# The products with the values in a chunk-band attention: by query tile of four heads instead of by pairs of heads

## The chip, the cores and the metric

The kernel runs on one core of a Trainium2 chip. The metric is the device time of one execution in microseconds. TensorE (PE) does the products and the transposes; its loads of stationary operands are shown apart (PEld). VectorE (DVE), ScalarE (ACT) and GpSimd (POOL) compute, and SyncE (SP) issues most DMAs. Each engine works through its own list of instructions in the order in which it stands and waits on semaphores for the others.

## The reference

One layer of a hybrid encoder on 1024 tokens of width 1024. Both mixers read one normalised input and one combined projection. The first is an attention of 8 heads of width 64 over a band of the own chunk of 64 tokens and the 8 chunks before it, with a learned bias by distance; the second a gated delta rule of 4 heads of width 128, a recurrence over chunks. Then come an output projection and a feed-forward part. Cut to what matters here:

```
scores = einsum('bcqhd,bckhd->bchqk', qc, kb) * Dh**-0.5 + bias
scores = where(valid, scores, finfo(float32).min)
p = softmax(scores, axis=-1)
o = einsum('bchqk,bckhd->bcqhd', p, vb)          # the products with the values
...
h = h + concat([rms_norm(o_att), o_dn]) @ w_out
h = h + square(relu(rms_norm(h) @ w_ff1)) @ w_ff2
```

## The kernel before, in words

The span falls into three parts: projections (to about 365 us), the two mixers side by side (365 to 575 us), and the output projection and feed-forward part (from 575 us, L931 and later), whose large products take more than half of the span.

In the middle part three generators are run in turns by `interleave` (L263): the attention (L706), `delta_all` (the recurrence, L687) and the rest of the projection of the values. A generator yields the TensorE time that it has just put down, and the one that lies furthest back goes next. That gives the program's order; within it a scheduler sets each engine's list by priority, by a simulated timeline: what comes earlier in the program has the higher priority, and what isn't ready is passed by something behind it. The list of an engine is thereby fixed when the kernel is built. `tc.issue_after(x)` keeps what is put down inside it from being placed ahead of the instruction x; `tc.high_priority()` puts what is inside ahead of everything else that is ready.

The attention works by group g of four heads (two groups) and query tile t of 128 tokens (eight tiles): 16 units, named t00 to t17 in the program's names. Each is worked in two pairs of heads, pp = 0 and 1, with e the head of the pair:

- `start` (L761) has q of the tile loaded (two DMAs on SP, two buffers).
- `score` (L797) makes the products q k of one pair (L793): one PSUM bank for the newest keys of both heads (t_sb), one for each head's older keys (t_sa); VectorE adds bias and finds the maximum (L808, L817), ScalarE takes exp (L823, L826). The results are t_pb (both heads) and t_pa (one for each head).
- `value` (L831) turns them so that keys lie on the partitions: transposes of t_pb (L844, t_tpb), copied by ScalarE (L847, t_tb); transposes of t_pa (L855, t_tpa), copied by ScalarE for e = 0 (L860) and by VectorE for e = 1 (L858). Then the products with the values (L865, t_o): for each key tile j and each head one product with 64 columns of stationary values, so that the two heads of a pair write the two halves of the partitions of one PSUM bank. In the trace each product is two records, and 128*64 is the part of the array that it uses.
- `finish` (L869) copies t_o (L884), transposes it back (L887) and scales it by the sums (L888; in the second group also L893, L895), and `turn` (L898) makes the finished tile the left operand of the output projection (L904).

Before, the loop (L908) goes over 32 pairs: scores of one pair, then the values of the pair before it, and after the second pair `finish`. The transposes go through two PSUM banks (`ps_t`), the scores through three (`ps_a`), the products with the values through one (`ps_o`).

The delta part has names c_ and m_: c_pk, c_pv, c_pq, c_pS, c_mt and c_po are its full-size products (L461), c_tpv, c_tpq and c_tpo its transposes (L465); m_p and m_tp (L568 to L592) are small products on 32 or 64 rows and columns.

Of the kernel before, what the change touches and what calls it, by code (L numbers as in the profile page):

```python
# [14 lines left out]
P = 128  # L15
# [3 lines left out]
NT = SEQ // P  # L19
# [27 lines left out]
def hymba_kernel(  # L47
# [20 lines left out]
    nc = tc.nc  # L68
# [16 lines left out]
    def page(tag, name, dt=F32, w=512):  # L85
        return pools[tag].tile([P, w], dt, tag=tag, name=name, bufs=slots[tag])
# [14 lines left out]
    def bank(pool, name):  # L101
        return pool.tile([P, 512], F32, tag="bk", name=name)
# [380 lines left out]
    turned = [[], []]  # L483
# [7 lines left out]
    def delta_prep(kT, ab):  # L491
# [54 lines left out]
        for dst, src in ((x_dr, xd), (y_dr, ad)):  # L546
            for h in range(4):
                nc.sync.dma_start(out=dst[:, :, h, :], in_=src.rearrange("(q h) r e -> h q r e", h=4)[h])

    def delta_merge(c, res):  # L550

        n = f"m{c}"
# [153 lines left out]
    def attention(after):  # L706
# [54 lines left out]
        def start(g, t):  # L761
            n = f"t{g}{t}"
            T = dict(n=n, k0=max(0, t - 4))
            T["kb"] = max(0, t - 1)
            if (g, t) == (1, 1):
                T["q"] = [page("on", f"{n}_q{m}", F32R) for m in range(2)]
                for r0 in (0, 64):
                    for m in range(2):
                        nc.sync.dma_start(out=T["q"][m].bitcast(F32)[r0:r0 + 64], in_=q_dr[t, :, m, g, :])
            else:  # L770
                q = page("x", n + "_q", F32R, w=DM)
                qf = q.bitcast(F32)
                for r0 in (0, 64):
                    nc.sync.dma_start(out=qf[r0:r0 + 64].rearrange("p (m c) -> p m c", m=2), in_=q_dr[t, :, :, g, :])
                T["q"] = [part(q, m) for m in range(2)]
            T["sums"] = small("t", n + "_sum", 8)
            T["nm"] = small("t", n + "_nm", 8)
            T["s"] = {}
            tiles[g, t] = T
# [48 lines left out]
            T["s"][pp] = sa, sb  # L828
            return cost

        def value(g, t, pp):  # L831
            T = tiles[g, t]
            n, k0, kb = (T[k] for k in ("n", "k0", "kb"))
            na, nb = kb - k0, t + 1 - kb
            if pp == 0:
                T["po"] = bank(ps_o, n + "_o")
            po = T["po"]
            sa, sb = T["s"].pop(pp)
            T["spare"] = sb
            tp = bank(ps_t, f"{n}_tpb{pp}")  # L840
            for e in range(2):
                for j in range(nb):
                    c = e * 256 + 256 - (nb - j) * P
                    nc.tensor.transpose(tp[:, c:c + P], sb[:, c:c + P], ident)  # L844
            tb = page("raw", f"{n}_tb{pp}", w=516)
            w3 = [t_[:, 0:512].rearrange("p (a b) -> p a b", a=2)[:, :, 256 - nb * P:256] for t_ in (tb, tp)]
            nc.scalar.copy(*w3)  # L847
            ta = [None, None]
            if na:
                for e in range(2):  # L850
                    i = 2 * pp + e
                    tp = bank(ps_t, f"{n}_tpa{i}")
                    for j in range(na):
                        js = slice(j * P, (j + 1) * P)
                        nc.tensor.transpose(tp[:, js], sa[e][:, js], ident)  # L855
                    ta[e] = page("u", f"{n}_ta{i}")
                    if e:
                        turned[1].append(nc.vector.tensor_copy(ta[e][:, 0:na * P], tp[:, 0:na * P]).ins)  # L858
                    else:
                        turned[0].append(nc.scalar.copy(ta[e][:, 0:na * P], tp[:, 0:na * P]).ins)  # L860
            for j in range(na + nb):
                for e in range(2):
                    h = 4 * g + 2 * pp + e
                    c = j * P if j < na else e * 256 + 256 - (na + nb - j) * P
                    nc.tensor.matmul(po[64 * e:64 * e + 64, pp * P:(pp + 1) * P], vt[k0 + j][:, 64 * h:64 * h + 64],  # L865
                                     (ta[e] if j < na else tb)[:, c:c + P], start=(j == 0), stop=(j == na + nb - 1))
            return (na + nb) * 650

        def finish(g, t):  # L869
            T = tiles.pop((g, t))  # L870
# [34 lines left out]
                                    bc_row(again), ALU.mult)  # L905
            return 500

        units = [(g, t, pp) for g in range(2) for t in range(NT) for pp in range(2)]  # L908
        lag, late = 1, 2
        for i in range(len(units) + lag + late):  # L910
            if i < len(units):
                g, t, pp = units[i]
                if pp == 0:
                    start(g, t)
                    if (g, t) == (0, 2):
                        load_rest()
                    if (g, t) == (0, 6):
                        load_new(1)
                        load_old(1)
                yield score(g, t, pp)  # L920
            if lag <= i < len(units) + lag:
                g, t, pp = units[i - lag]
                yield value(g, t, pp)
                if pp:
                    yield finish(g, t)
            if i >= lag + late:
                g, t, pp = units[i - lag - late]
                if g and pp:
                    yield turn(t)

    def out_proj():  # L931
# [476 lines left out]
```

## Time and profile before

| | |
|---|---|
| median of 3 runs | 1288.59 us (1287.44 to 1289.28) |
| profiled execution | 1288.31 us |
| its span | 1286.6 us |
| TensorE busy | 1260.6 us, 98% |
| VectorE busy | 935.0 us, 73% |
| ScalarE busy | 553.9 us, 43% |
| granted TensorE clock, mean | 0.998 |

The profile is one execution. A busy TensorE is one that has records under way; matmuls overlap, and a record's duration is its passage through the pipeline. What a record costs is seen in the distance between the starts of neighbours. Times in the views are in microseconds from the start of the span. In brackets behind a row stands the idle time ahead of it on its engine and what ended it.

### The profile page before, as it was taken

What the parts mean: (1) busy time and instruction counts of PE and PEld (TensorE: products, weight loads), DVE (VectorE), ACT (ScalarE), POOL (GpSimd) and SP (SyncE); (2) the same over time, 40 slices, a digit from 0 to 9 for tenths busy, and PEclk for the clock granted to TensorE, in tenths of its full rate; (3) what the DMA queues carried; (4) which work ended last, traced back from release to release, by engine and by line L of the source; (5) the groups of instructions that cost most, each with busy time, mean ns of one, the idle gap of its engine ahead of it and who ended that gap; (6) DMA issues with size and microseconds to landing.
All of it is one profiled execution on the core that took longest, in us unless ns stands there. A gap on an engine that the chain in (4) does not pass through costs nothing.

```text
span 1286.6 us, 18043 instructions
## 1 busy us (share of the span) xinstructions
PE 1260.6 (98%) x6702; PEld 1040.6 (81%) x6702; DVE 935.0 (73%) x1401; ACT 553.9 (43%) x919; POOL 293.0 (23%) x499
## 2 busy tenths in 40 slices
PE   9999999999999999989999999999999999999998
PEld 7778878788888887868877788888887888888886
DVE  7899987665046666863529876776668997897988
ACT  7233132133166664665335445444455443333331
POOL 4435461454024355523310000000000000000034
PEclk9999999999999999999999999999999999999999
DMA  6214353656492742125351433232358733422002
GB/s 223 61 44 140 100 164 112 145 147 160 144 270 79 218 109 75 42 65 163 122 166 31 151 116 129 98 110 97 105 196 318 238 93 104 131 86 95 17 33 98
DMA packets 129288, 160.65 MB, mean 125 GB/s; under 512 B 22832, under 2 KB 71984, under 8 KB 128688
## 3 DMA queue, kind: packets, MB, share of 16 engines
q1 hardware_dynamic: 111104, 137.20, 34.7%
q10 hardware_dynamic: 18096, 22.29, 5.0%
q8 instruction: 53, 0.87, 0.3%
q14 instruction: 35, 0.29, 0.1%
HBM read 111.75 MB, written 47.71 MB: 124 GB/s over the span
## 4 chain that ended last, share of the span: by engine, by line
PE 72%; DVE 8%; issue 2%; DMA 2%; POOL 1%; ACT 1%; POOLq 1%; SPq 0%; ACTq 0%; DVEq 0%
PE q L1087 22%; PE p L1183 20%; PE op L166 5%; PE av_ps L166 3%; PE aq_ps L166 3%; PE g_ps L166 3%; PE t_o L865 3%; PE ak_ps L166 2%; PE t_sb L793 1%; PE t_sa L793 1%; PE t_tpb L844 1%; PE t_tpa L855 1%; PE c_mt L461 1%; PE c_pS L461 1%; DVE ml L148 1%
## 5 line engine op out<-in xcount | busy, mean ns | idle before, releaser
L1255 POOL TENSOR_TENSOR y<-y,y 128x1024 f32<-128x1024 f32 x6 | 19.3, 3243 | 591.7 <-DVE y L1251 572.9
L1251 DVE TENSOR_TENSOR y<-y,p 128x1024 f32<-128x1024 f32 x46 | 55.2, 1218 | 5.4 <-PE p L1183 4.5
L808 DVE CUSTOM_DVE_ANT_0 t_pb<-t_sb,biasn 128x256 f32<-128x256 f32 (+1 forms) x64 | 25.4, 402 | 43.6 <-POOL biasn L720 25.4
L166 PE MATMUL op<-mh,wo_h 128*128 128x512 f32 x128 | 50.3, 393 | 0.8 <-DVE t_nm L808 0.3
L166 PE MATMUL op<-ml,wo_h 128*128 128x512 f32 x128 | 50.1, 391 | 0.0
L166 PE MATMUL op<-mh,wo_l 128*128 128x512 f32 x128 | 48.3, 391 | 0.0
L823 ACT ACTIVATE t_pb<-t_pb,t_nm 128x256 f32<-128x256 f32 (+1 forms) x64 | 31.6, 494 | 22.7 <-DVE t_nm L817 12.7
L966 DVE TENSOR_TENSOR h<-op,op_x 128x512 f32<-128x512 f32 x16 | 10.8, 688 | 30.7 <-PE op L166 30.7
L793 PE MATMUL t_sb<-ks,t_q 128*128 128x256 f32 (+1 forms) x144 | 30.4, 308 | 0.8 <-DMA t_q<-q_dr 0.5
L973 POOL TENSOR_TENSOR op_q<-op_q 128x512 f32<-128x512 f32 x14 | 20.1, 1439 | 48.0 <-ACT op_q L972 47.8
L166 PEld LDWEIGHTS op<-mh,wo_h 128*128 128x128 f32 x128 | 24.0, 188 | 7.4 <-issue 1.0
L817 DVE CUSTOM_DVE_ANT_0 t_pa<-t_sa,biaso,t_nm 128x384 f32<-128x384 f32 (+2 forms) x48 | 26.3, 547 | 4.4 <-PE t_sa L793 2.9
L865 PE MATMUL t_o<-t_ta,vt 128*64 128x128 f32 x240 | 27.3, 293 | 1.4 <-DVE t_ta L858 1.1
L166 PEld LDWEIGHTS op<-mh,wo_l 128*128 128x128 f32 x128 | 24.0, 188 | 5.2 <-issue 0.2
L166 PEld LDWEIGHTS op<-ml,wo_h 128*128 128x128 f32 x128 | 24.0, 188 | 4.9
L166 PE MATMUL g_ps<-uh,wg_h 128*128 128x512 f32 x64 | 25.2, 394 | 1.4 <-ACT wg_h L147 1.4
L826 ACT ACTIVATE t_pa<-t_pa,t_nm 128x384 f32<-128x384 f32 (+2 forms) x48 | 26.4, 550 | 0.1
L793 PE MATMUL t_sa<-ks,t_q 128*128 128x256 f32 (+2 forms) x128 | 25.5, 310 | 0.3 <-DVE t_nm L808 0.3
L166 PE MATMUL g_ps<-uh,wg_l 128*128 128x512 f32 x64 | 25.2, 394 | 0.4 <-POOL wg_l L148 0.4
L166 PE MATMUL dq_ps<-uh,wdq_h 128*128 128x512 f32 x64 | 25.5, 398 | 0.0
L166 PE MATMUL dv_ps<-uh,wdv_l 128*128 128x512 f32 x64 | 25.4, 397 | 0.0
L166 PE MATMUL aq_ps<-waq_h,uh 128*128 128x512 f32 x64 | 25.3, 401 | 0.0
(1102 smaller groups left out, 4353.8 us busy)
## 6 DMA issues: line engine op xcount, KB each, us to landing
wa<-in_w_ff_dram SPq DMA_DIRECT2D x32, 512.0 KB
a<-in_w_ff_dram SPq DMA_DIRECT2D x32, 512.0 KB
b<-f_dr SPq DMA_DIRECT2D x32, 512.0 KB
f_dr<-yy ACTq DMA_DIRECT2D x16, 512.0 KB
t_q<-q_dr SPq DMA_DIRECT2D x30, 256.0 KB
f_dr<-zz ACTq DMA_DIRECT2D x13, 512.0 KB
ks<-k_dr SPq DMA_DIRECT2D x16, 256.0 KB
wo_r<-in_w_out_dram SPq DMA_DIRECT2D x16, 256.0 KB
```

The source lines that it names most:

```text
L166: nc.tensor.matmul(ps, a, b, start=(i == 0), stop=(i == n - 1))
L461: nc.tensor.matmul(ps[:, hs], lhs(h, hs), rhs(h, hs), start=True, stop=True)
L793: nc.tensor.matmul(o, q[m][:, i * P:(i + 1) * P], k[:, c], start=(m == 0), stop=(m == 1))
L808: nc.vector.tensor_tensor_reduce(sb[:, c], bk[:, c], new[g][pp][:, c], -1.0, 3.0e38, ALU.add, ALU.min, nm[:, 4 + i:5 + i])
L817: nc.vector.tensor_tensor_reduce(sa[e][:, 0:wa], bk[:, 0:wa], old[g][i][:, 384 - wa:384], -1.0, nm[:, 4 + i:5 + i], ALU.add, ALU.min, nm[: ...
L823: nc.scalar.activation(sb[:, c], sb[:, c], AF.Exp, bias=m, scale=-1.0, accum_out=T["sums"][:, 4 + i:5 + i])
L826: nc.scalar.activation(sa[e][:, 0:wa], sa[e][:, 0:wa], AF.Exp, bias=m, scale=-1.0, accum_out=T["sums"][:, i:i + 1])
L865: nc.tensor.matmul(po[64 * e:64 * e + 64, pp * P:(pp + 1) * P], vt[k0 + j][:, 64 * h:64 * h + 64], (ta[e] if j < na else tb)[:, c:c + P], ...
L973: nc.gpsimd.tensor_tensor(acc, acc, sq, ALU.add)
L1087: nc.tensor.matmul(part(ps, q), l[:, s], r, start=(k + m == 0), stop=(k == 3 and m == 2))
L1183: nc.tensor.matmul(part(ps[q], 0) if by_rows else part(ps[q // 2], q % 2), l[:, s], part(r, k), start=(i + k + m == 0), stop=(i + k + m == 4))
L1251: nc.vector.tensor_tensor(y[i][m], y[i][m], ps[m], op)
```

## The change

`value` now takes a whole tile. It first puts down the transposes and copies of all four heads and then the products of all four, through a new helper `held`: the first product is placed as the scheduler would have it, and all others are kept from being placed ahead of it and have high priority, so that they follow it at once. The order of the products is reversed in pairs and heads: pair 1 before pair 0, and head e = 1 before e = 0, so that the first product is that of the fourth head. The loop goes over 16 tiles: scores of the first pair of a tile, values of the tile before, its `finish`, then the scores of the second pair, then `turn`.

```diff
+    def held(args, step):
+        first = step(*args[0])
+        with tc.issue_after(first.ins), tc.high_priority():
+            for a in args[1:]:
+                step(*a)
...
-        def value(g, t, pp):
+        def value(g, t):
...
-            if pp == 0:
-                T["po"] = bank(ps_o, n + "_o")
-            po = T["po"]
-            sa, sb = T["s"].pop(pp)
...
+            po = T["po"] = bank(ps_o, n + "_o")
+            tbs, tas = [], []
+            for pp in range(2):
+                sa, sb = T["s"].pop(pp)
...
-            for j in range(na + nb):
-                for e in range(2):
-                    h = 4 * g + 2 * pp + e
-                    c = j * P if j < na else e * 256 + 256 - (na + nb - j) * P
-                    nc.tensor.matmul(po[64 * e:64 * e + 64, pp * P:(pp + 1) * P], vt[k0 + j][:, 64 * h:64 * h + 64],
-                                     (ta[e] if j < na else tb)[:, c:c + P], start=(j == 0), stop=(j == na + nb - 1))
-            return (na + nb) * 650
+            def add(pp, j, e):
+                h = 4 * g + 2 * pp + e
+                c = j * P if j < na else e * 256 + 256 - (na + nb - j) * P
+                return nc.tensor.matmul(po[64 * e:64 * e + 64, pp * P:(pp + 1) * P], vt[k0 + j][:, 64 * h:64 * h + 64],
+                                        (tas[2 * pp + e] if j < na else tbs[pp])[:, c:c + P],
+                                        start=(j == 0), stop=(j == na + nb - 1))
+
+            held([(pp, j, e) for pp in (1, 0) for j in range(na + nb) for e in (1, 0)], add)
+            return (na + nb) * 1300
...
-        units = [(g, t, pp) for g in range(2) for t in range(NT) for pp in range(2)]
-        lag, late = 1, 2
+        units = [(g, t) for g in range(2) for t in range(NT)]
+        late = 1
...
+                yield score(g, t, 0)
+            if 0 < i <= len(units):
+                yield value(*units[i - 1])
+                yield finish(*units[i - 1])
+            if i < len(units):
+                yield score(g, t, 1)
```

On TensorE the middle of the first group, tile t06 (queries 768 to 895 of heads 0 to 3), stood before as follows, from the older keys' transposes of its first pair on:

```order
L855 MATMUL t_tpa_5525<-ident,t_pa_5310 128x128 x3
L855 MATMUL t_tpa_5531<-ident,t_pa_5317 128x128 x3
L461 MATMUL c_pk<-state_298,kT_594 128x128 x4
L865 MATMUL t_o<-t_ta_5529,vt_3799 64x128
L844 MATMUL t_tpb_5578<-ident,t_pb_5492 128x128 x4
L865 MATMUL t_o<-t_ta_5535,vt_3799 64x128
L865 MATMUL t_o<-t_ta_5529,vt_3802 64x128
L865 MATMUL t_o<-t_ta_5535,vt_3802 64x128
L865 MATMUL t_o<-t_ta_5529,vt_3813 64x128
L865 MATMUL t_o<-t_ta_5535,vt_3813 64x128
L865 MATMUL t_o<-t_tb_5523,vt_3816 64x128 x2
L865 MATMUL t_o<-t_tb_5523,vt_3819 64x128 x2
```

One product of the first pair stands alone between c_pk and the second pair's t_tpb; the other nine follow, and the second pair's ten come twelve rows later. The same tile in the changed order, from the older keys' transposes of its last two heads on:

```order
L865 MATMUL t_tpa_5575<-ident,t_pa_5504 128x128 x3
L465 MATMUL c_tpv<-ident,c_jv 128x128 x4
L865 MATMUL t_tpa_5581<-ident,t_pa_5511 128x128 x3
L575 MATMUL m_p_4580<-m_yb,m_ab 32x32 x4
L465 MATMUL c_tpq<-ident,c_jq 128x128 x4
L575 MATMUL m_p_4580<-m_yb,m_ab 32x32 x4
L875 MATMUL t_o<-t_ta_5585,vt_3741 64x128
L875 MATMUL t_o<-t_ta_5579,vt_3741 64x128
L875 MATMUL t_o<-t_ta_5585,vt_3744 64x128
L875 MATMUL t_o<-t_ta_5579,vt_3744 64x128
L875 MATMUL t_o<-t_ta_5585,vt_3755 64x128
L875 MATMUL t_o<-t_ta_5579,vt_3755 64x128
```

The twelve short products and transposes of the delta part stand between the last transposes and the first product; the remaining fourteen of the tile's twenty products follow without anything between. The end of the middle part on TensorE, tile t17 (the last one), before:

```order
L844 MATMUL t_tpb_6572<-ident,t_pb_6464 128x128 x4
L855 MATMUL t_tpa_6579<-ident,t_pa_6476 128x128 x3
L855 MATMUL t_tpa_6585<-ident,t_pa_6483 128x128 x3
L865 MATMUL t_o<-t_ta_6583,vt_3802 64x128
L844 MATMUL t_tpb_6601<-ident,t_pb_6546 128x128 x4
L865 MATMUL t_o<-t_ta_6589,vt_3802 64x128
L865 MATMUL t_o<-t_ta_6583,vt_3813 64x128
L865 MATMUL t_o<-t_ta_6589,vt_3813 64x128
L865 MATMUL t_o<-t_ta_6583,vt_3816 64x128
L865 MATMUL t_o<-t_ta_6589,vt_3816 64x128
L865 MATMUL t_o<-t_tb_6577,vt_3819 64x128 x2
L865 MATMUL t_o<-t_tb_6577,vt_3822 64x128 x2
```

Products of the first pair stand between the transposes of the first and those of the second. The same place on TensorE in the changed order:

```order
L852 MATMUL t_tpb_6572<-ident,t_pb_6434 128x128 x4
L865 MATMUL t_tpa_6579<-ident,t_pa_6446 128x128 x3
L865 MATMUL t_tpa_6585<-ident,t_pa_6453 128x128 x3
L852 MATMUL t_tpb_6591<-ident,t_pb_6540 128x128 x4
L865 MATMUL t_tpa_6598<-ident,t_pa_6552 128x128 x3
L865 MATMUL t_tpa_6604<-ident,t_pa_6559 128x128 x3
L875 MATMUL t_o<-t_ta_6608,vt_3744 64x128
L875 MATMUL t_o<-t_ta_6602,vt_3744 64x128
```

All twenty transposes of the tile stand in a row, and the twenty products directly behind them.

## Rows read from the trace of the kernel before

**Rows 1.** The page's line of engines: busy us, share of the span, instructions.

```profile
PE 1260.6 (98%) x6702; PEld 1040.6 (81%) x6702; DVE 935.0 (73%) x1401; ACT 553.9 (43%) x919; POOL 293.0 (23%) x499
```

**Rows 2.** Stretches: us, busy of PE, PEld, DVE, ACT, POOL, clock, DMA share, GB/s.

```profile
365.00:463.00 98.00, 97.47 (x963) 83.55 (x962) 60.25 (x207) 61.85 (x190) 35.13 (x92) 1.00 0.56 163
463.00:540.00 77.00, 73.77 (x690) 64.10 (x689) 55.51 (x156) 46.75 (x136) 42.86 (x110) 1.00 0.29 78
540.00:575.00 35.00, 30.09 (x247) 23.36 (x247) 24.24 (x64) 21.65 (x59) 10.19 (x32) 0.95 0.13 40
553.40:556.80 3.40, 3.40 (x21) 2.41 (x21) 2.88 (x8) 1.78 (x5) 0.00 (x0) 0.50 0.00 0
...
620.00:1287.00 667.00, 656.14 (x2904) 541.96 (x2902) 515.83 (x441) 285.56 (x291) 38.94 (x17) 1.00 0.36 121
```

**Rows 3.** The tile t_o: records, duration in ns (min/median/max), first and last start.

```profile
L865 PE MATMUL t_o<-t_tb,vt x240: 272/273/411, 365.6 to 573.3; 128*64 128x128 f32 x120
...
L865 PE MATMUL t_o<-t_ta,vt x240: 272/273/476, 379.2 to 572.9; 128*64 128x128 f32 x120
```

**Rows 4.** Timeline of PE: start, us, engine, line, operation, array, moving tile, records.

```profile
407.13 0.88 PE L865 MATMUL t_o<-t_ta,vt 128*64 128x128 f32 x12
407.84 0.61 PE L865 MATMUL t_o<-t_tb,vt 128*64 128x128 f32 x8
408.38 0.51 PE L793 MATMUL t_sb<-ks,t_q 128*128 128x256 f32 x2
```

**Rows 5.** Timeline of PE, 468.4 to 471.7 us.

```profile
468.72 0.66 PE L844 MATMUL t_tpb<-ident,t_pb 128*128 128x128 f32 x4
469.22 1.06 PE L461 MATMUL c_pv<-c_jv,m_yb 128*128 128x128 f32 x8
470.11 1.06 PE L461 MATMUL c_mt<-c_jq,kT 128*128 128x128 f32 x8
471.10 0.66 PE L865 MATMUL t_o<-t_tb,vt 128*64 128x128 f32 x8
471.68 0.50 PE L793 MATMUL t_sb<-ks,t_q 128*128 128x256 f32 x2
```

**Rows 6.** Timeline of PE, 437.3 to 439.6 us.

```profile
437.32 0.43 PE L865 MATMUL t_o<-t_ta,vt 128*64 128x128 f32 x2
437.69 0.65 PE L844 MATMUL t_tpb<-ident,t_pb 128*128 128x128 f32 x4
438.27 0.76 PE L865 MATMUL t_o<-t_ta,vt 128*64 128x128 f32 x9
...
439.51 0.44 PE L855 MATMUL t_tpa<-ident,t_pa 128*128 128x128 f32 x2
```

**Rows 7.** Timeline of all engines at the last tile, 566.8 to 572.3 us.

```profile
566.89 0.55 PE L855 MATMUL t_tpa<-ident,t_pa 128*128 128x128 f32 x3 [0.35 <-ACT t_tb L847]
...
567.54 1.47 DVE L895 TENSOR_SCALAR t_on<-t_on,t_r 128x512 f32<-128x512 f32 x1 [1.86 <-POOL t_r L143]
...
568.93 0.55 DVE L858 COPY t_ta<-t_tpa 128x384 f32<-128x384 f32 x1
...
569.53 0.76 PE L865 MATMUL t_o<-t_ta,vt 128*64 128x128 f32 x9 [1.15 <-DVE t_ta L858]
...
570.77 0.87 PE L855 MATMUL t_tpa<-ident,t_pa 128*128 128x128 f32 x6
...
571.68 0.56 DVE L858 COPY t_ta<-t_tpa 128x384 f32<-128x384 f32 x1 [0.40 <-PE t_tpa L855]
...
572.29 0.52 PEld L865 LDWEIGHTS t_o<-t_ta,vt 128*64 128x64 f32 x9 [0.22 <-DVE t_ta L858]
```

**Rows 8.** Waits of PE, 360 to 575 us: total us, times, longest us.

```profile
PE t_sb L793 <- DMA t_q<-q_dr: 0.5, 1, 0.5
```

**Rows 9.** Timeline of PE ahead of the dip of the clock, 550.9 to 554 us.

```profile
550.96 0.66 PE L844 MATMUL t_tpb<-ident,t_pb 128*128 128x128 f32 x4 [0.87 <-DVE mixa L904]
...
553.20 0.80 PE L855 MATMUL t_tpa<-ident,t_pa 128*128 128x128 f32 x3 [0.79 <-ACT t_tb L847]
```

## The prediction: what the change does to the time

> **What bounds the kernel now.** I read the page first: TensorE is busy 98% of the span, VectorE 73%, ScalarE 43% [rows 1]. A kernel like this becomes shorter if TensorE gets less work or wastes less of it, and longer if something makes TensorE wait. Then I cut the span into stretches [rows 2]. The attention lies between 365 and 575 us. From 365 to 463 TensorE is busy 97.47 of 98.00 us: work taken off it there should come off the time nearly in full. From 463 to 540 it is busy 73.77 of 77.00, and from 540 to 575 30.09 of 35.00, so 3.2 and 4.9 us are waits, and there a saving can turn into a longer wait. [...] After 575 nothing is edited; from 620 to 1287 TensorE is busy 656.14 of 667.00, so an earlier start of that part is an earlier end.
>
> The products with the values are 480 records of 272 to 273 ns median, the first block at 365.6 us and the last ending after 573.3 [rows 3]. A record's duration is its passage through a pipeline and says nothing of its price; that is read from the distance of the starts. In the block at 407.13, 12 records take until 407.84 and 8 more until the next group at 408.38: 1.25 us for 20 [rows 4]. In the block at 471.10, 8 records take 0.58 us [rows 5]. The 12 more cost 0.67 us, 0.056 us each, so 8 alone are 0.45 us, and 0.13 us is paid for leaving the block. Entering costs too: eight c_pv, followed by a group of the same shape, take 0.89 us from start to start, 0.111 each, while eight c_mt, followed by products that use 64 of the array's columns, take 0.99 [rows 5]: 0.10 us. The first group behind a block pays a third time: four t_tpb after products take 0.50 us, though four records of 0.111 are 0.44 [rows 5]: 0.06 us. Together about 0.30 us for going to the products' array shape and back, 0.15 a change of shape, whatever the block's length.
>
> Some blocks are worse. At 437.32 two records, one product of one head, stand alone and the next group starts 0.37 us later, 0.26 over 0.111; their rest at 438.27 is 18 records, 1.24 us to the next group, where 18 records of 0.056 and the exit of 0.13 make 1.14 [rows 6]. So a lone first product costs some 0.10 more than a plain block's two ends, and its companion 0.10 more: 0.20 us.
>
> **How often.** In the order of TensorE's trace I count 51 unbroken blocks of these products: 27 up to 461 us, 15 up to 540, 9 after it. 19 of them are such lone products, from 379.2 to 567.4 us (11, 5 and 3 by stretch). In the changed order there are 16 blocks, 8, 5 and 3, none lone: every tile's 8 to 40 records follow each other. Over the whole stage the order's array shape changes 170 times before and 110 times after; the 35 blocks that go would give 70, but ten are given back elsewhere, where small products of the delta part now stand between full-size ones.
>
> **The change part by part.** The arithmetic is the same: the same transposes, copies and products, so no engine gets less in instructions. Gained on TensorE: 60 changes at 0.15 us are 9.0, 19 lone products at 0.20 are 3.8, together 12.8 us of TensorE's time. By stretch in proportion to the blocks and lone products that go (19 and 11, 10 and 5, 6 and 3): 7.1, 3.6 and 2.1 us.
>
> Against it stands the wait of a block for its last copy. The first product of the block is that of the fourth head, whose transposes VectorE copies last, and everything else on TensorE that is issued behind it stands behind it. In the last tile before, transposes at 570.77 end at 571.64, the VectorE copy starts at 571.68 and takes 0.56, and weights for its products load at 572.29 [rows 7]: 0.65 us uncovered, if VectorE is free. It was not so at 569.53: the copy began only at 568.93, behind an L895 of 1.47 us, and TensorE stood 1.15 us [rows 7]. In the changed order other work stands between the last transposes and the block in most tiles of the first stretch, as t06 shows, twelve short products and transposes, some 1 us at about 0.1 each; two (t03, t07) have only about 0.9, which the copy's own 0.65 and its turn on VectorE may exceed. For these I charge 0.9 us together. In t14, t15, t16 and t17 the block stands directly behind the last transposes: 0.65 each. In t17 all 20 transposes stand in a row, through two banks, so that from the third group on each waits for a copy out of PSUM: six copies of about 0.55, four of them on ScalarE, are 2.2 us on ScalarE alone, against 20 transposes of 0.11 us; some 1.5 us of wait, where the same tile before had 1.15 and 0.35 [rows 7]. I take these as equal.
>
> In the first stretch: 7.1 - 0.9 = 6.2. In the second: 3.6, less t14's 0.65, and less a quarter of the gain, 0.9, since 3.2 us of waits there show that chains through VectorE and ScalarE set the time in places, and a saving ahead of such a wait is lost; 2.05. In the third: 2.1 - 3 x 0.65 = 0.15, rounded to nothing, because here TensorE already waits 4.9 us. Sum 8.2 us.
>
> What is moved besides: the scores of a tile's second pair now follow the values of the tile before, so q stays in its two buffers longer and the load of the next but one starts later. TensorE waited for such a load once, 0.5 us [rows 8]; I price the move between nothing and four such waits, 2 us, and take nothing, since the load is issued a whole tile ahead. SP also issues the small loads of the delta part a few places later, behind keys and values; TensorE's waits in the first stretch, 0.5 us in all, leave no room for seeing it. The copy of the finished tile and its two transposes come once per tile as before. A tile's transposed probabilities are now held for four heads instead of two, in pages that exist already.
>
> [...] Between 540 and 575 us VectorE is busy 24.24 and ScalarE 21.65 of 35.00 us [rows 2], and TensorE's waits there are for their copies [rows 7]. [...]
>
> **The rivals.** (A) All of it is kept: the copies are covered by other work, because the waits of the second and third stretch are for other things; 12.8 us, and with the dip of the clock gone as well (3.40 us at half clock [rows 2], 1.7 us) 14.5: 1274 to 1276. For it: TensorE is the bound in two thirds of the stage. Against it: four blocks without cover. (B) Nothing comes of it: the delta part's chain, whose steps take turns on TensorE, VectorE and ScalarE, sets the end of the stage at 575, and a saved 8 us only becomes waits; 1288. For it: 8.1 us of waits from 463 on [rows 2]. Against it: 97.47 of 98.00 busy before. (C) Slower: every one of the 16 blocks is held up by its last copy with all else behind it, as long as the worst wait before, 1.15 us [rows 7]: 18.4 us, less 12.8, is 5.6 more, 1294. It decides where the mean wait of a block is over 12.8 / 16 = 0.8 us. For it: the 0.65 us of the quietest case lie near, and VectorE, busy 55.51 of 77.00, often has something in front of the copy. Against it: at ten of the blocks 1 us or more of other work lies between. (D) The clock: before the dip TensorE did transposes and waited, four t_tpb at 550.96 after 0.87 us idle, and three t_tpa at 553.20 after 0.79 [rows 9]; the change gathers transposes, so each of the last four tiles could have such a dip, 1.7 us, 6.8 in all: 1288.3 - 8.2 + 6.8 = 1286.9, and 1287.2 by the median. [...]
>
> **How the numbers follow.** The profiled execution took 1288.31 us (span 1286.6), 0.28 under the median of the runs, 1288.59. 1288.3 - 8.2 = 1280.1, by the median 1280.4. Likeliest, with a chance of 0.60: 1277 to 1285, from the whole gain of the first stretch and most of the second (11) to half of it (4). A 0.13, B 0.10, D 0.05, C 0.12. The range reaches from A's time to no change: 1274.5 to 1288.5; C is left out, and little else. About 0.2%, 2.6 us, is what can be told from no change here. Faster by more: the likeliest and A, 0.73. Within it: B and D, 0.15. Slower: C, 0.12.
>
> **What would show it.** Blocks of products in TensorE's trace fall from 51 to 16, with no lone ones, and TensorE's busy time by some 10 us in the stage; the first stretch is shorter by about 6 us up to the same tile; t14 to t17 show 0.5 to 0.8 us of wait of t_o for the VectorE copy of t_ta. If busy time falls but the stage ends as late as before, B holds; if t_o's waits sum to over 12 us, C; if the granted clock shows more dips, D. The forecast is wrong if the price of a shape change is not saved when blocks are joined.

## The result, and the profile after

The changed kernel takes 1294.78 us (median of 6 runs, 1292.04 to 1296.71), the kernel before 1288.21 (6 runs, 1287.44 to 1289.28): a ratio of 1.0048, interval 1.0033 to 1.0063. It is slower by 6.6 us, where 8.2 us of gain were forecast. The profiled execution took 1296.71 us, the longest of the six, with a span of 1294.9; before it was 1288.31 and 1286.6.

The stretches of the changed kernel, with the columns and bounds of [rows 2], and a short one behind the stage's end:

```profile
365.00:463.00 98.00, 94.89 (x975) 85.58 (x975) 59.73 (x199) 62.57 (x184) 40.87 (x105) 0.98 0.58 173
463.00:540.00 77.00, 71.65 (x693) 64.59 (x692) 56.39 (x169) 47.00 (x141) 40.00 (x109) 0.98 0.24 67
540.00:575.00 35.00, 24.43 (x192) 20.12 (x194) 22.91 (x61) 20.58 (x58) 8.45 (x22) 0.90 0.12 39
575.00:579.00 4.00, 4.00 (x41) 3.60 (x38) 1.01 (x2) 0.89 (x3) 0.00 (x0) 0.59 0.63 194
```

TensorE is now idle 3.1, 5.4 and 10.6 us in the three stretches, against 0.5, 3.2 and 4.9 in [rows 2], and the granted clock is below 1.00 in each. To compare like with like, the stage is cut from the first c_pk to the last product with the values. Before, in the columns of [rows 2]:

```profile
364.66:573.60 208.94, 200.26 (x1893) 170.19 (x1891) 140.13 (x427) 130.02 (x383) 88.52 (x233) 0.99 0.39 111
```

And after:

```profile
365.52:578.49 212.97, 193.93 (x1893) 173.02 (x1891) 140.04 (x428) 130.36 (x382) 88.79 (x236) 0.96 0.38 112
```

The same 1893 records, 6.3 us less busy, and yet 4.0 us longer. The clock hides a part of the saving. Its dips in the stage of the changed kernel, in the same columns:

```profile
459.63:466.46 6.83, 6.83 (x41) 6.27 (x41) 2.82 (x10) 3.13 (x9) 0.00 (x0) 0.50 0.27 80
541.55:544.97 3.42, 3.42 (x18) 3.37 (x18) 1.92 (x8) 2.90 (x10) 1.78 (x6) 0.50 0.02 5
562.03:565.45 3.42, 3.42 (x32) 3.09 (x29) 1.24 (x4) 1.49 (x5) 0.00 (x0) 0.50 0.02 5
575.69:578.49 2.80, 2.80 (x29) 2.47 (x25) 0.52 (x1) 0.00 (x0) 0.00 (x0) 0.50 0.73 206
```

At half clock TensorE was busy 16.5 us, before 3.4 [rows 2]. If work takes twice as long there, half of each is what the lower clock costs: 8.2 against 1.7 us. (A kernel below, nohold, bears this out: with 10.2 us at half clock and about as many blocks as before, 50, it comes to the same work in this way, 198.70.) So the work at full clock is 198.55 us before (200.26 - 1.71) and 185.71 after (193.93 - 8.23): 12.8 us less. Idle time went from 8.7 to 19.0, 10.4 more; the clock took 6.5 more. Less 12.8, plus 10.4 and 6.5, each rounded, is the stage's 4.0 us. The profiled span is 8.3 longer: 0.9 us of it lies ahead of the stage, where nothing is edited, and 3.4 behind it, 1.7 of that another dip, 3.4 us long at 995.5.

Where in the stage this comes about is seen when it is divided at t14's last product, before and after:

```profile
364.66:534.40 169.74, 166.05 (x1609) 142.84 (x1607) 111.26 (x353) 104.86 (x315) 73.68 (x191) 1.00 0.44 127
534.40:573.60 39.20, 34.21 (x285) 27.35 (x285) 28.87 (x74) 25.17 (x68) 14.84 (x42) 0.96 0.14 41
```

```profile
365.52:533.48 167.96, 160.00 (x1615) 144.16 (x1613) 111.44 (x355) 105.28 (x312) 77.36 (x202) 0.98 0.44 127
533.48:578.49 45.01, 33.94 (x281) 28.86 (x279) 28.60 (x73) 25.08 (x71) 11.44 (x35) 0.89 0.18 55
```

Up to there the changed kernel is 1.8 us shorter: 9.5 us less work, against 4.3 more idle time and 3.4 for the one dip, at 459.63. From there on it is 5.8 longer: 3.4 us less work, against 6.1 more idle time and 3.1 more for the clock.

What TensorE waited for between 360 and 585 us (total, times, longest):

```profile
PE t_o L875 <- DVE t_ta L868: 5.6, 5, 2.9
PE t_sb L800 <- DVE t_nm L824: 3.9, 3, 1.6
PE t_tpa L865 <- ACT t_tb L856: 2.5, 3, 1.7
PE t_sb L800 <- DMA t_q<-q_dr: 2.0, 1, 2.0
PE c_pk L461 <- DVE c_jv L620: 1.5, 1, 1.5
```

The prediction had a price for the first row (0.65 us in each of the last four tiles, 0.9 for two of the first group) and one for a part of the third, which it took as equal to before; it had taken the fourth as nothing, and the second and the last it had not. The block of t14 looks as expected, TensorE's timeline as in [rows 4]:

```profile
529.89 0.55 PE L865 MATMUL t_tpa<-ident,t_pa 128*128 128x128 f32 x3
531.08 0.88 PE L875 MATMUL t_o<-t_ta,vt 128*64 128x128 f32 x12 [0.65 <-DVE t_ta L868]
531.79 0.61 PE L875 MATMUL t_o<-t_tb,vt 128*64 128x128 f32 x8
532.23 0.82 PE L875 MATMUL t_o<-t_ta,vt 128*64 128x128 f32 x12
532.88 0.61 PE L875 MATMUL t_o<-t_tb,vt 128*64 128x128 f32 x8
533.42 0.51 PE L800 MATMUL t_sb<-ks,t_q 128*128 128x256 f32 x2
```

Forty records take 2.34 us, 0.058 each with the exit, and the wait ahead is 0.65. t15 to t17 are where it goes wrong. At t16's scores, all engines:

```profile
554.70 0.49 DVE L908 TENSOR_SCALAR t_on<-t_on,t_r 128x512 f32<-128x512 f32 x1 [2.35 <-POOL t_r L143]
555.10 0.61 DVE L824 CUSTOM_DVE_ANT_0 t_pa<-t_sa,biaso,t_nm 128x384 f32<-128x384 f32 x1
...
555.78 0.50 PE L800 MATMUL t_sb<-ks,t_q 128*128 128x256 f32 x2 [1.59 <-DVE t_nm L824]
...
560.04 0.55 PE L865 MATMUL t_tpa<-ident,t_pa 128*128 128x128 f32 x3 [1.75 <-ACT t_tb L856]
```

And at the last tile:

```profile
571.12 1.47 DVE L908 TENSOR_SCALAR t_on<-t_on,t_r 128x512 f32<-128x512 f32 x1
571.37 0.55 PE L865 MATMUL t_tpa<-ident,t_pa 128*128 128x128 f32 x3 [0.42 <-ACT t_tb L856]
...
572.60 1.66 DVE L148 TENSOR_TENSOR ml<-mixa,mh 128x512 fp32r<-128x512 f32 x1
574.18 0.54 DVE L868 COPY t_ta<-t_tpa 128x384 f32<-128x384 f32 x1
...
574.78 0.88 PE L875 MATMUL t_o<-t_ta,vt 128*64 128x128 f32 x12 [2.86 <-DVE t_ta L868]
```

In both places VectorE's list holds L908, the scaling of the tile finished before, ahead of what TensorE needs. At t16 VectorE stands 2.35 us for GpSimd's t_r with the maxima of the second pair behind it. At t17 L908 and a split of a finished tile into two parts (L148) take 3.1 us together; the last transposes end at 571.92, and their copy starts only at 574.18, behind both.

### The profile page after: what moved, and what is told of

It is laid out like the page before. It is cut to its first block, busy times and chain, and to the rows that moved or that the text cites. A ratio compares the mean times of both kernels' runs of the same rounds, so it can differ in the third digit from the quotient of the medians.

```text
span 1294.9 us, 18037 instructions
## 1 busy us (share of the span) xinstructions
PE 1257.6 (97%) x6702; PEld 1045.5 (81%) x6702; DVE 933.8 (72%) x1401; ACT 554.0 (43%) x919; POOL 293.9 (23%) x499
## 4 chain that ended last, share of the span: by engine, by line
PE 71%; DVE 8%; DMA 3%; issue 2%; ACT 2%; POOL 1%; POOLq 1%; SPq 0%; DVEq 0%; ACTq 0%
PE q L1099 21%; PE p L1195 20%; PE op L166 5%; PE av_ps L166 3%; PE aq_ps L166 3%; PE g_ps L166 3%; PE t_o L875 2%; PE ak_ps L166 2%; PE t_sb L800 1%; PE t_sa L800 1%; DMA wa<-in_w_ff_dram 1%; PE t_tpb L852 1%; PE t_tpa L865 1%; PE c_po L461 1%; PE c_pk L461 1%
## 5 line engine op out<-in xcount | busy, mean ns | idle before, releaser
L800 PEld LDWEIGHTS t_sb<-ks,t_q 128*128 128x128 f32 x144 | 21.1, 192 | 8.8 <-DVE t_nm L824 4.5
```

The costliest lines, as they stand in the source:

```text
L800: nc.tensor.matmul(o, q[m][:, i * P:(i + 1) * P], k[:, c], start=(m == 0), stop=(m == 1))
```

## The experiments

All kernels below come from one source in which a tile's transposes and its products are two functions, and a setting chooses for each tile whether it goes by tile, held, as in the changed kernel, or by pairs, as before; as far as the setting is that of one of the two kernels, TensorE's order in the traces is that kernel's (only5's is that of before through t14's products, fill's that of the changed kernel up to t14). Each ran beside the kernel before. The stage's figures are of each profiled execution, between the marks used above: its length, idle time, busy time at half clock, work at full clock, and the time from t14's last product to t17's. One execution is not the median (early's took 1282.4, nohold's 1293.6 us).

| kernel | median us | ratio (interval) | stage | idle | half clock | work | t14 to t17 |
|---|---|---|---|---|---|---|---|
| before | 1288.2 | | 208.9 | 8.7 | 3.4 | 198.6 | 39.2 |
| changed | 1294.8 | 1.0048 (1.0033 to 1.0063) | 213.0 | 19.0 | 16.5 | 185.7 | 45.0 |
| nohold | 1290.8 | 1.0020 (1.0007 to 1.0034) | 212.1 | 8.2 | 10.2 | 198.7 | 41.7 |
| pair | 1281.8 | 0.9949 (0.9934 to 0.9963) | 204.6 | 12.9 | 3.4 | 190.0 | 39.5 |
| fill | 1294.0 | 1.0043 (1.0029 to 1.0058) | 210.1 | 14.7 | 3.4 | 193.7 | |
| early | 1278.3 | 0.9934 (0.9916 to 0.9951) | 202.9 | 9.0 | 6.8 | 190.4 | 37.7 |
| late | 1295.6 | 1.0057 (1.0042 to 1.0072) | 215.7 | 17.9 | 6.5 | 194.6 | 42.7 |
| only5 | 1296.8 | 1.0064 (1.0048 to 1.0080) | 216.0 | 15.5 | 6.7 | 197.2 | 45.7 |
| tail5 | 1284.7 | 0.9961 (0.9945 to 0.9977) | 204.7 | 13.2 | 6.8 | 188.1 | 36.5 |
| tail6 | 1284.5 | 0.9966 (0.9955 to 0.9977) | 203.7 | 13.8 | 3.4 | 188.2 | 38.6 |
| hold3 | 1284.3 | 0.9978 (0.9956 to 0.9999) | 206.1 | 13.6 | 6.6 | 189.2 | 44.6 |
| plain3 | 1285.1 | 0.9976 (0.9960 to 0.9992) | 206.1 | 10.2 | 10.2 | 190.8 | 41.0 |
| early_q | 1276.8 | 0.9915 (0.9900 to 0.9930) | 198.2 | 7.1 | 0 | 191.1 | 37.7 |
| mix_q | 1275.6 | 0.9902 (0.9886 to 0.9919) | 196.3 | 8.3 | 0 | 188.0 | 37.7 |
| after_pool | 1283.8 | 0.9964 (0.9947 to 0.9981) | 204.3 | 13.3 | 6.8 | 187.6 | 36.8 |
| mix_q_pool | 1272.6 | 0.9879 (0.9856 to 0.9901) | 193.1 | 5.9 | 0 | 187.3 | 35.8 |

**The hold taken off, and a hold by pairs.** nohold and pair:

```diff
-TILE = lambda g, t: ((1, 0), (1, 0), True)
+TILE = lambda g, t: ((0, 1), (0, 1), False)                  # nohold: pairs, heads, held
```

```diff
-MODE = lambda g, t: "tile"
+MODE = lambda g, t: "pair"                                   # pair
+PAIR = lambda g, t, pp: ((pp,), (1, 0), True)
```

> The changed kernel's loop by tile, but the products put down plainly, pair 0 first, without the hold and its priority; in the built order they lie in 50 blocks with 18 lone products, like before (51 and 19). Theory W (the joined blocks make TensorE wait for the last copy, and the lower clock follows such waits): with single products free to fill the waits, work, waits and clock are about those of before, 1286 to 1290 us. Rival L (the loop by tile is what costs: scores of the second pair and loads of q come later, whatever the products do): slow as the changed kernel, 1292 to 1296, with TensorE still waiting for t_nm and t_q.

> The loop of before by pairs of heads, with each pair's products held together (32 blocks, one lone product; array shape changes 161 in the built order against 199 before). Theory W: 38 changes at 0.15 and 18 lone products at 0.20 us are 9.3 us less work at full clock; a pair's block waits for its copy too, but with half as much behind it, so waits rise by 2 to 6 us: 1281 to 1286 us. Rival H (any hold costs more in waits than it saves): 1289 us or more. Rival L: the loop is that of before, so all of the 9.3 us is kept, 1279.

Without the hold the products lie in 50 blocks again and the work at full clock is that of before, 198.7 us: the saving belongs to the joined blocks. But the time is not back at that of before: 2.9 us remain, and in the profiled execution that is lower clock, 10.2 us at half clock against 3.4. So neither theory stood as put: the loop by tile costs by itself, less than rival L said. pair came out as theory W said, 1281.8: 8.6 us less work, 4.2 more idle.

**Products that only fill the wait.** fill:

```diff
+                if g and t >= 4:
+                    with tc.issue_after(T["last"].ins), tc.high_priority():
+                        for _ in range(FILLERS):
+                            nc.tensor.matmul(T["po"][:, 0:P], ident, ident, start=True, stop=True)
```

> The changed kernel with 8 more products of the identity with itself (0.9 us, into the bank that the block's first product overwrites) in the last four tiles of the second group, issued after the tile's last transpose, where TensorE waits for the copy. They compute nothing that is used. Theory W with the clock as a term of its own: the products lie inside the waits and the lower clock comes less often, by two or three dips of 3.4 us, 1.7 us each: 1289 to 1293 us. Rival K (the clock does not depend on what TensorE does there): the dips stay and the additional work costs 0 to 2 us, 1294 to 1297.

Inconclusive. The eight fillers are two records each and take 1.9 us, not 0.9, as TensorE's timeline has them at t14:

```profile
525.66 1.95 PE L905 MATMUL t_o<-ident 128*128 128x128 f32 x16
527.54 0.88 PE L884 MATMUL t_o<-t_ta,vt 128*64 128x128 f32 x12
```

Over four tiles that is 7.5 us more work. The time is 1294.0, at the lower end of rival K's range, over 12 runs of 1288.9 to 1296.7; the profiled execution, 1291.35 us, has one dip of 3.4 us in the stage where the changed kernel's had four, and the median of the runs' mean clocks is 0.9955 against 0.9925. It fits a clock that follows what TensorE does in the waits, but does not show it: the waits differ too, and one of the three dips that fill lacks is the one at the load of q, ahead of any filler, where both have the same order and a wait of 2.0 us.

**Where in the stage.** early, late and only5 choose the tiles that go in the changed form:

```diff
-MODE = lambda g, t: "tile"
+MODE = lambda g, t: "pair" if g else "tile"                  # early: first group only
+MODE = lambda g, t: "tile" if g else "pair"                  # late: second group only
+MODE = lambda g, t: "tile" if g and t >= 5 else "pair"       # only5: t15 to t17 only
```

> By tile and held in the first group of heads, by pairs and as before in the second. Theory W: in the first group 19 blocks and 11 lone products go, 7.1 us, against one wait of 0.5 and perhaps the load of q of 2.0 us; the second group is as before: 1281 to 1286 us. Rival L: the late load of q and the late scores cost as much in the first group, 1287 to 1290.

> The complement of the run in which only the first group was changed: first group by pairs as before, second group by tile and held. Theory W (in the second group, where little other work is left, the held blocks and the late scores make TensorE wait, and the lower clock follows): if the two halves add up, 1288 + (1295 - 1278) = about 1304 us; at least 1298. Rival X (the loss is an interaction: the first group ends earlier and the second collides with loads): not above 1294 us.

> As before, except the last three tiles (t15 to t17), which are by tile and held; 60 products stand behind the last delta record. Theory T: these three tiles carry the whole loss of the second group, 1294 to 1298 us, like the run with all eight tiles of that group changed (1295.6). Rival B: 3/8 of it, 1290 to 1292.

The first group alone gives 9.6 us (1278.3 against 1287.9 of the runs beside it). The second alone costs 7.2, short of the 16 that adding up would give: the first group's gain is worth little when the last tiles are in the changed form. And three tiles alone, t15 to t17, cost 7.7 us, as much as all eight. That is theory T's number, but for its reason the next pair tells otherwise.

**The last tiles by pairs.** tail5 and tail6 leave the changed form except for the last three or two tiles:

```diff
-MODE = lambda g, t: "tile"
+MODE = lambda g, t: "pair" if g and t >= 5 else "tile"       # tail5 (tail6: t >= 6)
```

> By tile and held, except the last three tiles (t15 to t17), which go by pairs as before. Theory T (what costs is how much attention is left when the delta part's work is used up: in the built order 60 of its products with the values stand behind TensorE's last delta record in the changed kernel, 40 before and here): 1276 to 1282 us, near the run with the whole second group as before. Rival B (each held block of the second group costs alike): five of the eight tiles' cost of 16.5 us stays, 1286 to 1290.

> As the run before, but only the last two tiles (t16, t17) go by pairs; t15 is held. 60 products stand behind the last delta record, as in the changed kernel. Theory T: the loss is back, 5 us or more above the run with three tiles by pairs, 1285 to 1291. Rival B: one more tile, 2 us more than that run.

Both are 10 us under the changed kernel: the last two tiles carry 10 of the 16.5 us between early and the changed kernel, and t10 to t14 the other 6 (4 by the ratios to the kernel before). But they are equal, 1284.7 and 1284.5, although 40 products stand behind the last delta record in one and 60 in the other. Theory T, by which that number decides, falls; rival B, an equal price for each held block, too, since two blocks of eight carry most of it.

A kernel with both pairs' scores in a row was meant to take away the waits of t_sb:

```diff
                 yield score(g, t, 0)
+                yield score(g, t, 1)
             if 0 < i <= len(units):
                 yield value(*units[i - 1])
                 yield finish(*units[i - 1])
-            if i < len(units):
-                yield score(g, t, 1)
```

> The changed kernel with the scores of both pairs of a tile one behind the other, and the values of the tile before it after them; products held as in the changed kernel. If the waits of t_sb for t_nm (3.9 us in the changed kernel) and part of the low clock come from the place of the second pair's scores, they go and the time falls by 4 to 7 us, to 1288 to 1291. If the held blocks alone cause the loss, 1293 to 1297 us.

It missed on all counts, 1323.67 us (ratio 1.0289, 1.0260 to 1.0317). The scheduler let the attention fall behind, so that the delta part's last record comes 164 us into the stage and 78 us are left with attention only. These columns are those of [rows 2]:

```profile
363.00:527.00 164.00, 149.31 (x1454) 131.75 (x1453) 100.60 (x309) 89.54 (x260) 79.70 (x207) 0.98 0.42 127
527.00:605.00 78.00, 56.10 (x444) 45.23 (x445) 38.65 (x118) 41.07 (x121) 10.16 (x32) 0.89 0.15 45
```

Without other work TensorE is busy 72% of the time, at a mean clock of 0.89: what a tile of this attention costs when nothing covers its chain.

**Loop or hold in the last tiles.** hold3 and plain3 are early with t15 to t17 by tile, held or not:

```diff
-MODE = lambda g, t: "pair" if g else "tile"
+MODE = lambda g, t: "tile" if not g or t >= 5 else "pair"                           # hold3, plain3
-TILE = lambda g, t: ((1, 0), (1, 0), True)
+TILE = lambda g, t: ((1, 0), (1, 0), True) if not g else ((0, 1), (0, 1), False)    # plain3
```

> The first group by tile and held, t10 to t14 as before, t15 to t17 by tile and held: the run with the second group as before (1278.3 us) with the changed form put back in the last three tiles alone. Theory V (in these tiles no delta work is left to cover the waits for copies and maxima): 6 to 10 us more, 1284 to 1288. If the loss of these tiles came only from t10 to t14 being late: 1278 to 1280.

> The same with the products of t15 to t17 put down plainly, without hold and priority. If the hold makes the loss of these tiles (TensorE waits for the copies ahead of a block): 1278 to 1281 us. If the loop by tile makes it (scores of the second pair after the values, their PSUM waiting for VectorE): as the held one, 1284 to 1288. Half each: about 1282.

Both are some 6 us above early, and equal to each other within their spread: by the medians the loop by tile is enough for the loss. The traces say otherwise. There the last three tiles take 37.7 us in early, 41.0 in plain3 and 44.6 in hold3, all three with the same order on TensorE up to t14, so the loop makes 3.3 us and the hold 3.6 more; nohold and the changed kernel, 41.7 and 45.0, are 3.3 apart. The plain kernel's longer time at half clock does not offset this: 6.8 of its 10.2 us lie behind the load of q, and in the last three tiles it has 3.4 against 6.6 of the held one. So the hold's share is not settled.

**The load of q.** In the second group's second tile q goes to two pages of the first group's biases, free only after that group's last scores; early_q takes other pages. tail5_q, mix_q, mix5_q and mix_q_pool have it too.

```diff
-                T["q"] = [page("on", f"{n}_q{m}", F32R) for m in range(2)]
+                T["q"] = [page("u", f"{n}_q{m}", F32R) for m in range(2)]
```

> First group by tile and held, second group as before, and q of the second group's second tile loaded into pages of the large pool instead of the two of the first group's biases, which are free only after that group's last scores. TensorE waited there 2.1 us for the load, with 6.8 us of low clock behind it in the profiled execution. If the load is early enough: 2 to 5 us less, 1274 to 1277 us; if it stands behind another wait in the queue, 1278 to 1279.

> The first of these kernels, and q of the second group's second tile loaded into pages of the large pool. If the two gains add: 1.5 us under it, 1274 to 1280 us, and it may be the fastest of all. If the held blocks of t10 to t14 cost waits that the load hid: no better than 1276.8, the run with the whole second group as before and this load.

TensorE's wait for t_q, 2.1 us in early, is gone, and with it the dip behind it. From 455 to 466 us of early_q:

```profile
455.00:466.00 11.00, 10.97 (x119) 9.85 (x117) 5.77 (x20) 5.15 (x16) 3.94 (x13) 1.00 0.68 197
```

None of the five kernels with this load has a dip there; of the nine without it that hold the first group's tiles in the changed kernel's loop, and wait 1.5 to 2.4 us for q, six have one. 1.5 us come off early, 5.3 off tail5 (1279.41, ratio 0.9929, 0.9913 to 0.9945), and 6.0 off mix (see the next kernels). With this load t10 to t14 by tile cost 2.6 us more than by pairs (tail5_q against early_q), not 6.

**Pairs held in the second group.** mix holds them in all its tiles, without and with the load; mix5_q leaves t15 to t17 unheld:

```diff
-PAIR = lambda g, t, pp: ((pp,), (0, 1), False)
+PAIR = lambda g, t, pp: ((pp,), (1, 0), True)                                          # mix, mix_q
+PAIR = lambda g, t, pp: ((pp,), (1, 0), True) if t < 5 else ((pp,), (0, 1), False)     # mix5_q
```

> First group by tile and held, second group by pairs, each pair held (24 blocks, no lone products). Theory W: in the second group a hold by pairs saves up to 16 blocks' worth less 8, 8 blocks and 8 lone products, 4.0 us of work, and costs 2 to 5 us of waits in the last tiles: 1276 to 1281 us, near the run with the second group as before (1278.3). Rival H (a hold in the second group always costs more than it saves): 1282 or more.

> The same with the pairs of t15 to t17 held as well. If a hold by pairs costs in the last tiles as the hold by tile does there: 1277 to 1280 us; if only the tile-wise form costs: 1273 to 1276.

> First group by tile and held; t10 to t14 by pairs, each pair held; t15 to t17 by pairs as before; early load of q of the second group's second tile. Five fewer lone products and blocks than the fastest run so far (1276.8): 1.5 to 2.5 us of work, if no waits come with them: 1274 to 1276 us.

mix took 1281.54 (0.9951, 0.9935 to 0.9966), just above W's range and below H's; mix5_q 1277.61 (0.9918, 0.9904 to 0.9933), a miss by 1.6; mix_q 1275.55. A hold by pairs costs nothing in the last tiles.

**VectorE's queue.** after_pool is the changed kernel with one operation on another engine, mix_q_pool the same in mix_q:

```diff
-                nc.vector.tensor_scalar(o, o, r, None, ALU.mult)
+                nc.gpsimd.tensor_scalar(o, o, r, None, ALU.mult)
```

> The changed kernel with the scaling of a finished tile of the second group (t_on by t_r) on GpSimd, which computes t_r, instead of VectorE. In the changed kernel's trace VectorE waits there for GpSimd and then works 0.5 to 1.5 us, with the maxima of t16's second pair and the last copy of t17 queued behind it; TensorE waits 1.59 and 2.86 us for these. Theory Q (VectorE's queue, not the copy itself, makes the waits of the last tiles): these two waits fall by 2 us or more together, 1289 to 1293 us. Rival: the waits are those of the chain through maxima, exp and copies, and stay; 1294 to 1297.

> The fastest kernel so far (1275.6 us), with the same scaling on GpSimd. Theory Q: its wait of 1.61 us at the last tile falls by 1 us or more, 1273 to 1275 us. Rival: 1275 to 1277.

Eight instructions moved, and the changed kernel is 11 us faster, 1283.8, beyond what theory Q expected. The two waits that were 1.59 and 2.86 us are gone or small, in its waits of TensorE from 360 to 580 us:

```profile
PE t_o L883 <- DVE t_ta L871: 2.7, 4, 0.9
...
PE t_sb L803 <- DVE t_nm L827: 1.0, 1, 1.0
```

and from t15 on no dip of the clock is left:

```profile
539.00:568.62 29.62, 24.33 (x229) 19.19 (x229) 20.99 (x57) 20.02 (x57) 11.97 (x25) 1.00 0.12 37
```

Of the 8.7 us that its stage is shorter, 5.8 are idle time and 4.8 the lower clock (16.5 - 6.8, halved), against 1.9 more work. In mix_q, where the scores go by pairs, the same edit gives 2.9 us. So this place in VectorE's queue costs the changed kernel some 8 us that it does not cost there, if the two may be subtracted. They may only roughly: the lists are built anew with the edit, and TensorE's order, too, differs in some twenty places from 482 us on. Neither the kernel before with this edit alone nor the changed kernel with this edit and the early load of q was run. mix_q_pool, 1272.6 us, is faster than both kernels by 1.2% and more.

## Why the prediction was wrong, point by point

**The price of a shape change** was right. The forecast was 12.8 us less work; the trace has 198.55 - 185.71 = 12.8 with the same records, in 16 blocks as read from the order. nohold, with 50 blocks, has none of it; pair, with 32, has 8.6 where 9.3 was expected, so that the agreement to a tenth is partly luck.

**The first stretch** was about right: 7.1 us of work and 6.2 in all were forecast; early, which changes that group alone, has 8.1 us less work and 2.0 more idle and lower clock in its profiled execution, and 9.6 us by the medians. In the changed kernel one term taken as nothing eats most of it: **the load of q**, the first of two steps that failed. "TensorE waited for such a load once, 0.5 us [rows 8]; I price the move between nothing and four such waits, 2 us, and take nothing, since the load is issued a whole tile ahead" was the wrong end: it waited 2.0 us, and 6.8 us at half clock followed, 3.4 more. The issue a tile ahead does not help where the pages come free only after the first group's last scores; with other pages the wait is gone, and 1.5, 5.3 and 6.0 us come off in three pairs of kernels. So at t14's last product the changed kernel was 1.8 us ahead, where 6.2 and 2.05, together 8.2, had been forecast. Of the 6.4 us missing there, the load of q makes 5.4. The second stretch did much as forecast: idle time between the last products of t07 and t14 went from 3.2 to 4.9 us, where 1.55 had been charged.

**The third stretch is the other step that failed**, as large: nothing was forecast, and the last three tiles took 5.8 us more, with 3.4 us less work and 9.2 more of waits and lower clock. "In t14, t15, t16 and t17 the block stands directly behind the last transposes: 0.65 each", with t17's row of transposes set against the waits before ("I take these as equal"), made 2.1 us of gain into nothing. It was 0.65 in t14 and t16, 0.98 in t15 and 2.86 in t17, and 3.0 us of waits of t_sb for maxima and 2.5 of t_tpa for t_tb came with it; the first of these two has no term in the sum. Nor has the lower clock behind the waits, 3.1 us more than before. 0.65 is the copy when VectorE is free; the prediction had the other case in its own rows, the copy behind an L895 of 1.47 us [rows 7], and used it only as the price in rival C. In the changed order that operation, which waits for GpSimd, stands ahead of the second pair's maxima and the last copy in VectorE's queue. after_pool shows it, as far as one edit with its newly built order can: without it there, the tiles from t14's end to t17's take 36.8 us, not 45.0.

**The rivals.** A had the whole saving right and the cover wrong. C came nearest in the time, 1294, but by luck: not 16 blocks waited 1.15 us each; there were five waits for the copy, 5.6 us, and 9.9 for four other things, most of it in three tiles. D had the size of the clock, 6.8 us against 6.5, at a chance of 0.05, and this is luck in part too, since half of it came at the load of q. It was put as a case of its own, beside C, while in the trace each dip comes behind long waits: 1.99 us ending at 458.8, 1.42 at 541.3, 1.75 at 560.0 with 0.65 at 561.2, and 2.86 at 574.8. The two belong in one case. That gathered transposes alone bring the dips is not borne out: early_q, mix_q and mix_q_pool make the same number of transposes, the first group's by whole tiles too, and have no dip in the stage. The third stretch lost its 5.8 us by a queue in front of the copies more than by the copies: with L908 on GpSimd, in after_pool, t14's end to t17's takes 36.8 us. B was wrong: the end of the stage did move.

What stays open: how much of the loss in the last tiles the hold makes, some 3.5 us by two pairs of traces and nothing by the medians of hold3 and plain3; and why a dip at about 12 us into the last part's products (995.5 us in the changed kernel) is in some profiled executions and not in others. It stands behind a wait of 1.8 us for p50b_l, ending at 994.4, but the kernel before has that wait too, ending at 987.8, and no dip there.

## What to carry to other kernels

Joining products of one array shape saves what the changes of shape cost, here 0.15 us each, but a saving in work counts only where other work fills the waits (here 12.8 us less of it ended 6.6 us slower): cut the stage at the point where the filler runs out, and price the last tiles by themselves. For each wait that a change adds, read the whole queue of the engine that ends it, not the duration of the one instruction; an operation that waits for a third engine in that queue is paid by everyone behind it: here VectorE stood 2.35 us for t_r, and TensorE 1.59 for the maxima behind. Where the lower clock follows idle TensorE, the wait is paid twice, here 10.4 us more idle time and 6.5 more for the clock, so a wait and its dip belong in one sum.

## What the runs showed of the hardware

Going to a product on half of the array's columns and back costs about 0.30 us as read from [rows 4, 5] (0.10 on the way in, 0.13 out, 0.06 at the group behind). The way out costs alike in blocks of 8, 20 and 40 records: they take 0.58, 1.25 [rows 4, 5] and 2.34 us to the next group, which at 0.055 a record leaves 0.14 to 0.15. With 0.20 us for each lone first product this held as a sum over a stage: 12.8 us forecast and 12.8 measured in the changed kernel, 9.3 and 8.6 in pair, 7.1 and 8.1 in early. The granted clock fell to 0.50, for 3.4 or 6.8 us, shortly behind four of the changed kernel's longest waits (1.99, 1.42, 1.75 and 2.86 us), but not behind two others as long, of t_sb (1.59 us, ending at 555.8) and c_pk (1.51, at 514.1). Nor did it follow fill's wait for q (1.98, at 457.2), though up to there fill and the changed kernel, with 1.99, have the same order. So the lower clock often comes behind a long wait here, but not always. The same VectorE scaling of 512 columns took 0.49 us at 554.70 and 1.47 at 571.12, where GpSimd worked beside it (two operations of L148 from 571.04, 2.67 us together). That the neighbour is the reason is not shown: at 480.82 the scaling took 0.48 us beside a GpSimd operation (L474, 1.32 us from 480.89), too.
